# A decoder trunk of two layers: each reciprocal square root computed by one GpSimd instruction in place of eleven VectorE instructions

## The chip, the cores and the metric

The kernel runs on one core of one Trainium2 chip. The core has five engines that work side by side, each on its own queue of instructions and in the order of that queue: TensorE (PE; its weight loads stand apart as PEld), VectorE (DVE), ScalarE (ACT), GpSimd (POOL) and SyncE (SP), which here only issues transfers. They meet at semaphores. The metric is the device time of one execution in microseconds (us); lower is better.

## The reference, cut to what matters

A sequence of 256 tokens with 1024 features passes through two layers. Layer 0 mixes tokens by softmax attention heads (q and k normalised) and by Mamba-2 heads (a chunked scan, then a gated norm over groups of 512 features). Layer 1 mixes them by a gated delta rule (q and k normalised to length one, the output of each head normalised). After each mixer come a gated MLP with a short convolution, and an embedding that is gated by the sigmoid of a normalised residual. Each normalisation ends in one reciprocal square root:

```python
def rmsnorm(x, gain):
    xf = x.astype(jnp.float32)
    y = xf * lax.rsqrt(jnp.mean(xf * xf, axis=-1, keepdims=True) + EPS)
    return (y * gain.astype(jnp.float32)).astype(x.dtype)

def l2norm(x):
    return x * lax.rsqrt(jnp.sum(x * x, axis=-1, keepdims=True) + EPS)
```

The four other places (the group norm of the Mamba heads, the norm of a delta-rule head's output, and q and k in either layer) have the same form.

## The kernel before

All matrices stream once from memory, in blocks of up to 128 x 1024 numbers (`piece`, L133). ScalarE cuts each block to its high part (`whi`, L155), VectorE subtracts to get the low part (`wlo`, L156), and TensorE multiplies three times for each 128 x 128 tile and its 256 columns of activations (`mm3`, L174; L181 to L183). Four buffers each hold raw blocks, high parts and low parts. The residual `x` stays feature-major in eight tiles.

The norms are applied late. `norm_tile` splits `x` times the gain for the next product at once, while ScalarE squares the tiles and GpSimd adds the squares up (L241; in the very first norm VectorE does). `norm_end` (L244) sums over the partitions by four small matmuls into `nps`, VectorE scales (`st`, L251), `rsqrt` (L185) makes `rtok`, two numbers for each of 128 partitions, and two TensorE transposes (`rep`, L263) and a ScalarE copy spread it into `Rrep`, by which each product is multiplied when it leaves PSUM. So TensorE may go on with products before the norm is known, as far as its order of instructions lets it.

`rsqrt` takes the reciprocal square root of a small tile of 2, 4 or 32 columns: two integer instructions make a first guess (L189, L191), and three Newton steps of three instructions each follow (L197, L198, L199), all on VectorE and each needing the one before. It is called 25 times:

- six times in `norm_end`, with 2 columns: before layer 0, before and after each MLP, before layer 1;
- once in layer 0 for all q and k heads, with 32 columns (`_even`), and twice for the two groups of Mamba heads, with 2 columns;
- sixteen times in layer 1 (`_odd`), with 4 columns: eight times in `prep` for the lengths of k and q of a pair of heads (`rkq`), eight times in `core` for the output of the pair (`ro`).

In layer 1 `prep(kh)` projects and convolves q and k, transposes them (`pkq`), takes their squares, and builds from `rkq` the coefficients `cs`, the matrix `L` (VectorE L846, GpSimd L848, ScalarE L850) and its first inverse `T` (VectorE L854), which TensorE then transposes (`pS`, L858) and improves in six doublings and two Newton steps. `core(kh)` runs the two chunks, normalises the output (`so`, the rsqrt, `ro2`, `on`, `oT`), and `gate` multiplies it by the gate. Two pairs are prepared ahead of the one in `core`.

The order on each engine is not that of the code: the framework schedules all instructions by its own estimate of their durations and writes them into each engine's queue. The splits of weights stand ahead by a priority of 80 places. An engine then never passes over an instruction that waits. The six zero blocks `zb` for the doublings are filled on GpSimd early in layer 0 (L465).

Of the kernel before, what the change touches and what calls it, by code (L numbers as in the profile page):

```python
# [7 lines left out]
F32 = mybir.dt.float32  # L8
# [24 lines left out]
# Columns of the packed per-feature vectors (feature on the partition).  # L33
# [8 lines left out]
# Columns of the constants that depend on shapes alone.  # L42
# [8 lines left out]
class Trunk:  # L51
    def __init__(self, ctx, tc, stream, xT, pT, pv, tok, cst, out):
        self.tc, self.nc, self.ctx = tc, tc.nc, ctx
        self.stream, self.out = stream, out
        self.off = 0
        self.order = []
        self.n = 0
        self.pshare, self.share = 0.0, 0.0
        nc = self.nc
        ep = ctx.enter_context  # L60
        self.cpool = ep(tc.tile_pool(name="cpool", bufs=1))
        self.rawp = ep(tc.tile_pool(name="rawp", bufs=4))
        self.splp = ep(tc.tile_pool(name="splp", bufs=4))
        self.smallp = ep(tc.tile_pool(name="smallp", bufs=3))
        self.chain = ""
        self.nrm = ep(tc.tile_pool(name="nrm", bufs=1, space=PSUM))

        warm = self.cpool.tile([P, 1], F32, tag="warm", name="warm")
        nc.vector.memset(warm, 0.0)
        nc.scalar.activation(warm, warm, AF.Exp)  # L70
        # matmuls on zeros: TensorE's clock is up when the first operands arrive
        zt = self.cpool.tile([P, 256], F16, tag="zt", name="zt")
        nc.vector.memset(zt, 0.0)
        pz = self.nrm.tile([P, 512], F32, tag="nrm", name="pwarm")
        for _ in range(WARM):
            nc.tensor.matmul(pz[:, :T], zt[:, :P], zt, start=True, stop=True)
        self.pv = self.cpool.tile([P, NPV], F32, tag="pv", name="pv")
        nc.scalar.dma_start(self.pv, pv)
        xs = self.cpool.tile([P, KD, T], F32, tag="x", name="x")
        for m in range(0, KD, 2):  # L80
            nc.sync.dma_start(xs[:, m:m + 2], xT[:, m:m + 2])
        self.x = [xs[:, m] for m in range(KD)]
        self.tok = self.cpool.tile([P, 64], F32, tag="tok", name="tok")
        self.cst = self.cpool.tile([P, NCC], F32, tag="cst", name="cst")
        self.cst_src, self.tok_src = cst, tok
        self.pT = pT
        self.ones = self.cpool.tile([P, 1], F32, tag="ones", name="ones")
        nc.gpsimd.memset(self.ones, 1.0)
        self.ident = self.c("ident")
        self.id16 = self.cpool.tile([P, P], F16, tag="id16", name="id16")  # L90
        self.zb = [[self.cpool.tile([P, 4, P], F16, tag=f"zb{s}_{l}", name=f"zb{s}_{l}") for l in range(6)]
                   for s in range(1)]

# [13 lines left out]
    @contextmanager  # L107
    def psum(self, **banks):
        """The 8 PSUM banks of a phase, by the kind of work that rotates through them."""
        assert sum(banks.values()) <= 7  # L110
        with self.tc.tile_pool(name=self.uid("psum"), bufs=1, space=PSUM) as pool:
            self.psp, self.banks = pool, banks
            yield
# [12 lines left out]
    @contextmanager  # L126
    def on(self, chain):
        """Work of a chain of its own: its tiles don't wait for those of other chains."""
        was, self.chain = self.chain, chain
        yield  # L130
        self.chain = was

    def piece(self, blocks, lo=None):  # L133
        """Stream in weight blocks (array, layer, k0, nk, c0, nc), 1024 columns at a time, and split them."""
# [31 lines left out]
    def lo_engine(self, share):  # L166
        """GpSimd takes a share of the low halves, VectorE the rest."""
        self.pshare += self.share if share is None else share
        if self.pshare >= 1.0:
            self.pshare -= 1.0  # L170
            return self.nc.gpsimd
        return self.nc.vector

    def mm3(self, out, w, a, start=True, stop=True):  # L174
        """out += w.T @ a over k-tiles, w = (hi, lo) [128, nk, f], a = list of (hi, lo)."""
        nc = self.nc
        n = len(a)
        for k in range(n):
            wh, wl = w[0][:, k], w[1][:, k]
            ah, al = a[k]  # L180
            nc.tensor.matmul(out, wh, ah, start=start and k == 0, stop=False)  # L181
            nc.tensor.matmul(out, wh, al, start=False, stop=False)  # L182
            nc.tensor.matmul(out, wl, ah, start=False, stop=stop and k == n - 1)  # L183

    def rsqrt(self, src, n, dst=None):  # L185
        nc = self.nc
        s = self.small(n, "ri", I32)
# [15 lines left out]
    def split(self, src, hi, lo, scale=None):  # L203
        """hi + lo = src * scale, hi and lo of 12 significant bits."""
# [53 lines left out]
    def replicate(self, r, n, dst=None):  # L258
        """[128 tok, n] -> [128, n*128] with row values on every partition."""
# [92 lines left out]
    def conv4(self, pool, ps, w, b=None):  # L352
        """2 * silu(causal conv of R * ps), four taps, feature-major."""
# [20 lines left out]
    def softplus(self, x, n, dst):  # L374
        """max(x, 0) + log1p(exp(-|x|)) on a [128, n] tile; log1p by its atanh series."""
# [22 lines left out]
    def rowdram(self, col):  # L398
        """[128 tok, 32] -> [32, 128] in DRAM."""
# [15 lines left out]
    def _even(self, mp):  # L415
# [6 lines left out]
        # dt, decay sums  # L422
# [44 lines left out]
        # B, C, x  # L467
# [43 lines left out]
        def ssd(t):  # L511
            """heads 2t, 2t+1"""
# [28 lines left out]
        # q, k (feature-major), v (token-major)  # L541
# [69 lines left out]
        # attention  # L611
# [44 lines left out]
        # z gate, group norm  # L656
# [31 lines left out]
        # output projection  # L688
# [21 lines left out]
    def _odd(self, mp):  # L710
# [17 lines left out]
        # beta, decay sums  # L728
# [8 lines left out]
        # softplus(a + dt_bias) and softplus(-b) = -log(sigmoid(b))  # L737
# [47 lines left out]
        def prep(kh):  # L785
# [18 lines left out]
            # k stays as it is: 1 / |k| goes into the rows of the triangular system and its right sides,  # L804
            # and its solution times k needs none
# [10 lines left out]
            # Gram matrices  # L816
# [9 lines left out]
            # decays; index of a problem: chunk * 2 + head  # L826
# [25 lines left out]
            # inverse of the unit triangular L by doubling its blocks; T16 = inv(L), S16 = its transpose  # L852
# [36 lines left out]
            # two Newton steps in float32: S += S (I - L' S)  # L889
# [35 lines left out]
        def core(kh, st, bv):  # L925
            k2, qd, sq_, kt, Pm, S32, cs = st
            # chunk 0
# [10 lines left out]
            # chunk 1  # L938
# [11 lines left out]
            # outputs, token-major, index of a problem: chunk * 2 + head  # L950
# [7 lines left out]
            # normalisation over the value dim  # L958
# [198 lines left out]
```

## Time and profile before

| | us |
|---|---|
| median of 3 runs | 952.07 |
| the runs | 948.49, 952.07, 952.13 |
| span of the profiled execution, first to last instruction | 948.2 |
| TensorE busy | 903.1 (95%) |
| VectorE busy | 751.2 (79%) |
| ScalarE busy | 584.3 (62%) |
| GpSimd busy | 77.2 (8%) |

The profiled execution has a span and no device time of its own on record; its span is 0.3 under the fastest run and 3.9 under the median. The stages in the span: layer 0 mixer to about 205, MLP and embedding to 425, the delta rule to about 702, its output product, MLP and embedding to the end. A row of the timeline gives start, duration, engine, line, operation, result and operands, shape and number, and in brackets how long the engine had been idle and what it waited for. Rows of equal instructions that follow each other are merged ("x3").

### The profile page before, as it was taken

Reading aid. Unit: us, or ns where it says so; the run is one execution under the profiler, and the core shown is the slowest. Engines: PE = TensorE matmul, PEld = TensorE weight load, DVE = VectorE, ACT = ScalarE, POOL = GpSimd, SP = SyncE. Lnnn points to the kernel's source line nnn. Section 1 sums busy time; section 2 is a strip of 40 time slices with the busy share of each in tenths; the row PEclk is TensorE's granted clock in tenths of the full one; section 3 lists DMA queues with packets and bytes.
Section 4 is the critical chain, followed back from the end, with each engine's and each line's share of the span. In section 5 each row is a group of like instructions: output and inputs, shape, how many; then the busy total and the mean of one; then the engine's idle time right before and its main releaser. Section 6 shows DMA issues by size and latency. Waiting matters only on the chain.

```text
span 948.2 us, 19896 instructions
## 1 busy us (share of the span) xinstructions
PE 903.1 (95%) x7768; PEld 865.4 (91%) x7768; DVE 751.2 (79%) x1636; ACT 584.3 (62%) x1231; POOL 77.2 (8%) x83
## 2 busy tenths in 40 slices
PE   7979999999999999998989998999999999999998
PEld 5978778899999999987878898889899999999997
DVE  6767778888788766687889998999868888876665
ACT  5467656565655544664877777777745656654452
POOL 2000012110000001020111101111002000000100
PEclk9889999999999999999899999999999999999999
DMA  7544532456666555645333243322445555555562
GB/s 266 155 130 140 156 113 91 138 194 195 193 192 200 181 186 171 190 137 165 96 125 96 79 144 107 117 90 82 134 133 179 179 200 195 188 187 183 172 190 77
DMA packets 49822, 145.65 MB, mean 154 GB/s; under 512 B 9344, under 2 KB 15040, under 8 KB 49728
## 3 DMA queue, kind: packets, MB, share of 16 engines
q1 hardware_dynamic: 40608, 139.84, 46.7%
q10 hardware_dynamic: 9120, 4.53, 1.9%
q8 instruction: 61, 1.00, 0.4%
q14 instruction: 33, 0.27, 0.1%
HBM read 143.27 MB, written 1.08 MB: 152 GB/s over the span
## 4 chain that ended last, share of the span: by engine, by line
PE 75%; DVE 13%; DMA 4%; ACT 4%; issue 2%; POOL 1%; ACTq 0%; SPq 0%; POOLq 0%
PE pd L181 4%; PE pd L183 4%; PE pd L182 4%; PE pg L181 4%; PE pg L182 4%; PE pu L181 4%; PE pu L182 4%; PE pg L183 4%; PE pu L183 4%; DVE wlo L156 4%; DMA AC<-rowdr 2%; DMA GC<-rowdr 2%; PE pwo L182 2%; PE pgd L183 2%; PE pgd L181 2%
## 5 line engine op out<-in xcount | busy, mean ns | idle before, releaser
L156 DVE TENSOR_TENSOR wlo<-raw,whi 128x1024 fp32r<-128x1024 f32 (+2 forms) x266 | 323.5, 1217 | 89.1 <-ACT whi L155 85.6
L155 ACT ACTIVATE whi<-raw 128x1024 fp32r<-128x1024 f32 (+2 forms) x266 | 276.3, 1039 | 173.3 <-PE pd L182 46.3
L183 PE MATMUL pd<-yh,wlo 128*128 128x256 f32 x352 | 99.6, 283 | 0.0
L181 PE MATMUL pd<-yh,whi 128*128 128x256 f32 x352 | 99.6, 283 | 0.0
L182 PE MATMUL pd<-yl,whi 128*128 128x256 f32 x352 | 99.6, 283 | 0.0
L181 PE MATMUL pg<-xh,whi 128*128 128x256 f32 x352 | 97.3, 277 | 0.6 <-DVE x L1011 0.3
L181 PE MATMUL pu<-xh,whi 128*128 128x256 f32 x352 | 97.3, 277 | 0.0
L182 PE MATMUL pg<-xl,whi 128*128 128x256 f32 x352 | 97.3, 277 | 0.0
L183 PE MATMUL pg<-xh,wlo 128*128 128x256 f32 x352 | 97.2, 276 | 0.0
L182 PE MATMUL pu<-xl,whi 128*128 128x256 f32 x352 | 97.2, 276 | 0.0
L183 PE MATMUL pu<-xh,wlo 128*128 128x256 f32 x352 | 97.2, 276 | 0.0
L181 PE MATMUL pgd<-xh,whi 128*128 128x256 f32 x256 | 76.3, 298 | 0.3 <-DVE z L991 0.3
L182 PE MATMUL pgd<-xl,whi 128*128 128x256 f32 x256 | 74.9, 293 | 0.0
L183 PE MATMUL pgd<-xh,wlo 128*128 128x256 f32 x256 | 74.8, 292 | 0.0
L363 DVE SCALAR_TENSOR_TENSOR chh<-cg,pv,chh 128x255 f32<-128x255 f32 x132 | 66.7, 505 | 4.0 <-ACT chh L361 2.1
L183 PEld LDWEIGHTS pd<-yh,wlo 128*128 128x128 f32 x352 | 67.6, 192 | 0.0
L181 PEld LDWEIGHTS pd<-yh,whi 128*128 128x128 f32 x352 | 67.6, 192 | 0.0
L182 PEld LDWEIGHTS pd<-yl,whi 128*128 128x128 f32 x352 | 67.6, 192 | 0.0
L181 PEld LDWEIGHTS pg<-xh,whi 128*128 128x128 f32 x352 | 66.1, 188 | 0.8 <-issue 0.8
L182 PEld LDWEIGHTS pu<-xl,whi 128*128 128x128 f32 x352 | 66.1, 188 | 0.0
L183 PEld LDWEIGHTS pu<-xh,wlo 128*128 128x128 f32 x352 | 66.1, 188 | 0.0
L182 PEld LDWEIGHTS pg<-xl,whi 128*128 128x128 f32 x352 | 66.1, 188 | 0.0
(358 smaller groups left out, 2657.5 us busy)
## 6 DMA issues: line engine op xcount, KB each, us to landing
raw<-stream SPq DMA_DIRECT2D x232, 512.0 KB, 3.6
raw<-stream SPq DMA_DIRECT2D x32, 448.0 KB, 3.2
AC<-rowdr ACTq DMA_DIRECT2D x16, 128.0 KB, 4.0
GC<-rowdr ACTq DMA_DIRECT2D x16, 128.0 KB, 4.0
x<-xT SPq DMA_DIRECT2D x4, 256.0 KB, 5.0
out<-x SPq DMA_DIRECT2D x8, 128.0 KB, 1.8
cst<-cst SPq DMA_DIRECT2D x1, 645.0 KB, 6.4
raw<-pT SPq DMA_DIRECT2D x2, 256.0 KB, 2.5
```

The lines of the kernel that those rows point to most:

```text
L155: nc.scalar.activation(hi[:, :cols], raw[:, :cols], AF.Copy)
L156: self.lo_engine(lo).tensor_tensor(lo_[:, :cols], raw[:, :cols], hi[:, :cols].bitcast(F32), op=ALU.subtract)
L181: nc.tensor.matmul(out, wh, ah, start=start and k == 0, stop=False)
L182: nc.tensor.matmul(out, wh, al, start=False, stop=False)
L183: nc.tensor.matmul(out, wl, ah, start=False, stop=stop and k == n - 1)
L363: nc.vector.scalar_tensor_tensor(out=h[:, s:], in0=g[:, :T - s], scalar=w(3 - s), in1=h[:, s:], op0=ALU.mult, op1=ALU.add)
```

## The change

`rsqrt` issues one GpSimd `tensor_tensor` with the operation `pow` and returns; its second operand is a column of -0.5 that GpSimd writes once at the start. What stood in `rsqrt` before is no longer reached. The other differences are comments that were taken out; so line numbers rise by 2 after L88 and by 5 after `rsqrt`.

```diff
         self.ones = self.cpool.tile([P, 1], F32, tag="ones", name="ones")
         nc.gpsimd.memset(self.ones, 1.0)
+        self.mhalf = self.cpool.tile([P, 1], F32, tag="mhalf", name="mhalf")
+        nc.gpsimd.memset(self.mhalf, -0.5)
...
     def rsqrt(self, src, n, dst=None):
         nc = self.nc
+        o = dst if dst is not None else self.small(n, "ry")
+        nc.gpsimd.tensor_tensor(o, src, self.mhalf.to_broadcast([P, n]), op=ALU.pow)
+        return o
         s = self.small(n, "ri", I32)
         y = self.small(n, "ry")
```

The instructions of every engine are scheduled anew. Three places, each of before and then of after.

GpSimd, around the first norm (`rtok` is its result, `zb` the zero blocks, `xbc` a Mamba tile; the row `ISA` in the middle is a reload of GpSimd's instruction library, which the framework puts ahead of the first two-operand instruction):

```order
6 L88 MEMSET ones 128x1
7 L465 COPY zb_0_118<-id_117 128x512
8 L465 COPY zb_1_119<-id_117 128x512
9 L465 COPY zb_2_120<-id_117 128x512
10 L465 COPY zb_3_121<-id_117 128x512
11 L465 COPY zb_4_122<-id_117 128x512
12 L465 COPY zb_5_123<-id_117 128x512
13 L665 ISA
14 L665 TENSOR_TENSOR xbc_139_627<-xbc_139_627,z_451 128x256
```

```order
6 L88 MEMSET ones 128x1
7 L90 MEMSET mhalf 128x1
8 L470 COPY zb_0_120<-id_119 128x512
9 L470 COPY zb_1_121<-id_119 128x512
10 L470 COPY zb_2_122<-id_119 128x512
11 L190 ISA
12 L190 TENSOR_TENSOR rtok_259<-st_257,mhalf 128x2
13 L470 COPY zb_3_123<-id_119 128x512
14 L470 COPY zb_4_124<-id_119 128x512
15 L470 COPY zb_5_125<-id_119 128x512
```

The library load now stands directly ahead of the first `pow`, behind three of the six copies. On TensorE 22 more matmuls of the first z projection (`pz`) now stand ahead of the two `rep` transposes that wait for `rtok`; before, they stood behind them.

VectorE in the delta stage, around the norm of one pair's output (`st` are the small tiles ahead of the rsqrt and behind it, `cg` and `chh` steps of a convolution, `zb` a step of the doublings, `wlo` a low part):

```order
946 L970 TENSOR_SCALAR st_7689<-st_7687 128x4
947 L189 TENSOR_SCALAR ri_7691<-st_7689 128x4
948 L191 TENSOR_SCALAR ry_7692<-ri_7691 128x4
949 L197 SCALAR_TENSOR_TENSOR rt_7695<-ry_7692 128x4
950 L198 TENSOR_TENSOR rt_7696<-rt_7695,st_7689 128x4
951 L199 SCALAR_TENSOR_TENSOR ry_7697<-rt_7696,ry_7692 128x4
952 L197 SCALAR_TENSOR_TENSOR rt_7701<-ry_7697 128x4
953 L871 TENSOR_TENSOR zb_5_123<-pY_7433,cst 128x4x64
954 L198 TENSOR_TENSOR rt_7702<-rt_7701,st_7689 128x4
955 L363 SCALAR_TENSOR_TENSOR chh_7811<-cg_7809,pv,chh_7811 128x255
```

```order
747 L876 TENSOR_TENSOR zb_5_123<-pY_6657,cst 128x4x64
748 L972 SCALAR_TENSOR_TENSOR st_6911<-st_6904,st_6909 128x4
749 L975 TENSOR_SCALAR st_6913<-st_6911 128x4
750 L361 TENSOR_TENSOR cg_7266<-pgd_7241,Rrep_5420 128x256
751 L978 TENSOR_TENSOR st_6917<-ry_6915,sqs_6012 128x4
752 L376 SCALAR_TENSOR_TENSOR q_1409_6987<-cth_7020,chh_7015 128x256
753 L158 TENSOR_TENSOR wlo_7460<-raw_7457,whi_7459 128x1024
```

Before, the eleven steps are spread among the large instructions (the last of this rsqrt is row 962). After, the instruction that reads the result of `pow` (`st<-ry`) stands one instruction behind the one that makes its operand; over the sixteen calls of the stage there are none to three instructions between.

TensorE at the last norm (`nps` the sums over the partitions, `pgt` the gate product, `rep` the transposes that wait for `rtok`):

```order
7936 L248 MATMUL nps_13285<-ones,nss_13099 128x1
7937 L249 MATMUL nps_13285<-ones,nsq_13189 128x1
7938 L248 MATMUL nps_13285<-ones,nss_13099 128x1
7939 L249 MATMUL nps_13285<-ones,nsq_13189 128x1
7940 L181 MATMUL pgt_13331<-xh_12519,whi_13321 128x256
```

```order
7942 L254 MATMUL nps_12807<-ones,nsq_12711 128x1
7943 L183 MATMUL pgt_12833<-xh_12041,whi_12823 128x256
7944 L184 MATMUL pgt_12833<-xl_12042,whi_12823 128x256
7945 L185 MATMUL pgt_12833<-xh_12041,wlo_12824 128x256
7946 L183 MATMUL pgt_12833<-xh_12135,whi_12823 128x256
7947 L268 MATMUL rep_12817<-cst,rtok_12814 128x128 x2
```

Before, `rep` is row 7985: 45 matmuls stand between the sums and the transposes. After, there are four. The norm behind the first MLP and the one ahead of layer 1 have four as well (45 and 21 before), the two norms ahead of the MLPs nineteen, seven of them among the sums (33 before).

## Rows read from the trace of the kernel before

**Rows 1.** The page, busy time by engine: us (share of the span) xinstructions.

```profile
PE 903.1 (95%) x7768; PEld 865.4 (91%) x7768; DVE 751.2 (79%) x1636; ACT 584.3 (62%) x1231; POOL 77.2 (8%) x83
```

**Rows 2.** Windows: stretch, length, busy us of PE, PEld, DVE, ACT, POOL; clock, DMA.

```profile
205.00:385.00 180.00, 180.00 (x1559) 180.00 (x1559) 133.83 (x198) 99.94 (x149) 5.63 (x6) 1.00 0.59 186
...
425.00:702.00 277.00, 256.64 (x2480) 241.82 (x2480) 244.00 (x700) 200.91 (x562) 30.43 (x24) 0.98 0.37 111
```

**Rows 3.** Waits of PE, 425 to 702: waiter, awaited, us, times, longest.

```profile
PE pS L858 <- DVE T L854: 6.7, 7, 1.6
```

**Rows 4.** Timeline of VectorE, the first norm.

```profile
16.73 0.16 DVE L251 TENSOR_SCALAR st<-nps 128x2 f32<-128x2 f32 x1
...
21.80 0.16 DVE L199 SCALAR_TENSOR_TENSOR rtok<-rt,ry 128x2 f32<-128x2 f32 x1
...
28.62 0.42 DVE L486 TENSOR_TENSOR z<-pz,Rrep 128x256 f32<-128x256 f32 x1 [1.90 <-PE pz L183]
```

**Rows 5.** Timeline of GpSimd: three of six copies, and its first two-operand instruction.

```profile
15.55 3.75 POOL L465 COPY zb<-id 128x512 f16<-128x512 f16 x3 [14.72 <-ACT id L463]
...
64.06 0.99 POOL L665 TENSOR_TENSOR xbc<-xbc,z 128x256 f32<-128x256 f32 x1 [43.09 <-DVE xbc L538]
```

**Rows 6.** Timeline of PE, the first norm.

```profile
22.06 0.66 PE L263 MATMUL rep<-cst,rtok 128*128 128x128 f32 x2 [2.56 <-issue]
```

**Rows 7.** Windows behind the first norm, columns as in group 2.

```profile
22.00:26.00 4.00, 3.89 (x17) 3.59 (x18) 3.67 (x10) 2.05 (x4) 0.00 (x0) 0.50 0.41 141
```

**Rows 8.** The page, DMA issues: queue, count, KB each, median us to landing.

```profile
raw<-stream SPq DMA_DIRECT2D x1, 64.0 KB, 6.0
```

**Rows 9.** Timeline of ScalarE, its load of function tables.

```profile
1.17 1.28 ACT L70 ACT_TABLE_LOAD   x1 [1.17 <-PEq L1145]
```

**Rows 10.** Groups of GpSimd: form, count, busy us, mean ns, idle before.

```profile
L837 POOL TENSOR_TENSOR qd<-qd,q 128x256 f32<-128x256 f32 x8 | 6.2, 777 | 113.7 <-ACT qd L836 31.0 <-DVE q L371 25.9 <-DVE st L973 18.2
...
L88 POOL MEMSET ones<- 128x1 f32 x1 | 0.1, 98 | 0.3 <-POOLq L1145 0.3
```

**Rows 11.** Timeline of VectorE: steps of an rsqrt between large instructions, and in a chain.

```profile
497.30 0.16 DVE L198 TENSOR_TENSOR rt<-rt,st 128x4 f32<-128x4 f32 x1
497.37 0.16 DVE L191 TENSOR_SCALAR ry<-ri 128x4 int32<-128x4 int32 x1
...
551.25 0.17 DVE L189 TENSOR_SCALAR ri<-st 128x4 int32<-128x4 int32 x1
551.45 0.17 DVE L191 TENSOR_SCALAR ry<-ri 128x4 int32<-128x4 int32 x1
```

**Rows 12.** Timeline of GpSimd (first and third row) and of VectorE, delta stage.

```profile
474.70 1.28 POOL L848 TENSOR_TENSOR L<-L,cst 128x512 f32<-128x512 f32 x1 [15.05 <-DVE L L846]
...
474.88 2.18 DVE L156 TENSOR_TENSOR wlo<-raw,whi 128x1024 fp32r<-128x1024 f32 x1
...
570.78 2.53 POOL L848 TENSOR_TENSOR L<-L,cst 128x512 f32<-128x512 f32 x1 [14.04 <-DVE L L846]
```

**Rows 13.** Timeline of VectorE at the norm ahead of layer 1: first and last row.

```profile
421.60 0.16 DVE L251 TENSOR_SCALAR st<-nps 128x2 f32<-128x2 f32 x1 [1.18 <-PE nps L249]
...
424.03 0.16 DVE L199 SCALAR_TENSOR_TENSOR rtok<-rt,ry 128x2 f32<-128x2 f32 x1
```

**Rows 14.** Chain that ended last, 440 to 450: start, us, what.

```profile
442.47 6.90 DMA GC<-rowdr
```

**Rows 15.** Timeline of PE, then of VectorE, at the last norm.

```profile
919.68 0.36 PE L249 MATMUL nps<-ones,nsq 128*128 128x1 f32 x2
919.90 0.36 PE L181 MATMUL pgt<-xh,whi 128*128 128x256 f32 x1
...
920.08 0.16 DVE L251 TENSOR_SCALAR st<-nps 128x2 f32<-128x2 f32 x1 [1.42 <-PE nps L249]
```

**Rows 16.** Waits of the weight loads and of PE: waiter, awaited, us, times, longest.

```profile
PEld rep L263 <- issue: 5.2, 6, 2.7
...
PE pss L566 <- ACT sqk L563: 7.2, 3, 5.4
```

## The prediction

> **What bounds the kernel now.** I read the page first: TensorE is busy for 903.1 us of the span of 948.2, VectorE for 751.2, GpSimd for 77.2 [rows 1]. An average over stages says little, so the windows by stage come next. In the MLPs TensorE is busy for the whole stretch (180.00 of 180.00) and VectorE for three quarters of it; no reciprocal root stands there, and nothing can be won [rows 2]. In the delta stage, 425 to 702, TensorE is idle for 20.4 of 277 us and VectorE for 33.0: both are close to full, and sixteen of the 25 roots lie there [rows 2]. The waits of TensorE name what it is short of in that stage: 6.7 us, a third of its idle time, end on VectorE's `T`, which hangs on `rkq` [rows 3]. The other places are the six norms of the residual, where TensorE has to wait for `rep`. There it lost 5.2 us in all, 2.7 of them at the first norm [rows 16]. So TensorE sets the time, and a faster root is worth what it takes out of these waits: the waits for `T` and `rep`, and two long chains of small steps that start at a norm.
>
> **The part removed: eleven VectorE steps.** In a chain each starts 0.20 us behind the former; between large instructions a step pushes the next by 0.07 [rows 11]. There are 176 of them in the stage, and followed along the timeline they take 20.3 us of VectorE's queue, 0.115 each, so 1.27 for a root; the ends are 0.77 and 2.2.
>
> **The part added: one GpSimd `pow`.** The trace holds none. From below it costs a memset of one column, 0.10 us; from above the longest GpSimd row, 2.53 [rows 10, 12]. I take 0.78, the mean of the two-operand instruction of 256 columns, because the form is the same: far fewer columns speak for less, a power instead of a product for more [rows 10]. A handover costs 0.10: `rtok` ends at 21.96, `rep` starts at 22.06 [rows 4, 6]. To GpSimd and back a root takes 0.78 + 0.20 = 0.98 us.
>
> GpSimd also gets in VectorE's way. While it adds the identity to `L` (474.70, for 1.28), a subtraction `wlo` that started at 474.88 takes 2.18 us [rows 12]; it ends one ordinary subtraction after GpSimd does. I take it that a `pow` holds back in the same way what reads both operands from SBUF, as `wlo` does, and count only instructions that read PSUM as cover.
>
> At one place a rule of the Trainium skill speaks against the change: the page GPSIMD Engine Reference, section Engine selection, keeps two-operand elementwise work on VectorE, since GpSimd takes about twice as long. By that ratio on a step of 0.16 a `pow` would take an estimated 0.32, and the sum below would be some 5 us lower, not higher: the rule compares one instruction with one, and here one stands for eleven.
>
> **The delta stage.** VectorE's new order has none to three instructions between the operand and the reader of each root, 0.34 us on average over the sixteen, and I count half, 0.17, as cover. VectorE is thus held for 0.98 - 0.17 = 0.81 and freed of 1.27: 0.46 x 16 = 7.4 us of its queue. A third of TensorE's idle time ends on VectorE (6.7 of 20.4), so I pass on a third: -2.4. GpSimd's queue adds no wait that I can find: ahead of `rkq` stands `qd` of the same pair, which needs q, and so do the squares that `rkq` is made from. The chain from the squares to `T` gets shorter by about 6 us, but TensorE's order was written for that (some 60 matmuls between the last `pkq` and `pS` instead of some 100), so I count nothing for it.
>
> **The norm ahead of layer 1** starts the chain that ends in the landing of `GC` at 449.4, behind which TensorE is starved [rows 14]. From `st` to `rtok` it takes 421.76 to 424.19, 2.43 us [rows 13]; with `pow` 0.98. All of the 1.45 is on the path: -1.4.
>
> **The other norms.** Only four matmuls now stand between the sums and `rep` at three of them. At the last one the sums end at 920.04, `st` at 920.24, and the result would come at 921.22; four matmuls of 0.12 from 919.90 end by about 920.4 [rows 15]. TensorE idles 0.8 instead of the 0.5 of now ((5.2 - 2.7) / 5 [rows 16]): +0.9 for three. Two norms have twelve matmuls behind the sums, 1.4 us, which covers them: -1.0. Together -0.1. The roots of the attention and of the two groups lie beside other products; I count 0, with a us either way.
>
> **The first norm** is the place of the library load, which now stands right ahead of the first `pow`. Before, it had 43.09 us of idle time to hide in, so the trace bounds it by 0 and 43 [rows 5]. Two neighbours: a load of ScalarE's tables, 1.28 [rows 9], and a transfer of 64 KB from memory in these first microseconds, 6.0 [rows 8]. I take 6.0, since code for GpSimd has to come from memory. The copies end at 19.30 [rows 5], the load at 25.3, `rtok` at 26.1 instead of 21.96 [rows 4]. TensorE no longer loses the 2.56 at once, since 22 matmuls of `pz` stand ahead, but stops later all the same, and the granted clock of 0.50 (1.2 GHz) that followed the stop [rows 6, 7] comes again. Behind `rtok` hang the softplus, the decay sums and their trip through memory, at whose end TensorE waits 5.4 us [rows 16]. Part of the 4.1 us is made up, because VectorE had waited 1.90 for the second thing in that chain, the z product [rows 4], which is now partly done. Between 0 and +4.1 I take half: +2.0. With 1.28 instead of 6.0 `rtok` comes at 21.5, TensorE runs through at the higher clock (2.56, and some 26 matmuls at 0.12 instead of 0.21), and the term is -5.
>
> The Trainium skill has a price here: GPSIMD Engine Reference, section Instruction dispatch, puts the first call after such a load at about 6 us. By it the term stays at +2.0, and by the load of ScalarE's tables the whole sum would be 7 us lower. No row of this trace shows the load itself.
>
> **Sum:** -2.4 - 1.4 - 0.1 + 2.0 = -1.9 us, made against the span of 948.2. What lies around the span is not on record; the runs' median is 3.9 above it, and I carry the difference over to that: 952.1 - 1.9 = 950.2.
>
> **Rivals.**
> Slower: `pow` is long. Each further us costs 16 x 0.33 = 5.3 in the delta stage, 1 at layer 1, 3 to 5 at the other norms, about 0.5 at the first: some 11 us in all. From 0.78 + 0.6 = 1.4 us on the change is slower by more than 0.5%; at the 2.53 of the longest row it is +17, so 969. For it: a power is computed in many steps, and the scheduler left next to no cover. Against: GpSimd has only two to four columns to work on.
> Faster: the load is short, -5 for +2.0, so 943; or `pow` is close to the memset, -0.68 x 11 = -7.5, so 943 as well. For it: two columns are little work. Against: the transfers of that time are far from short.
> The roots were never what the delta stage waits for: its -2.4 falls away, 952.6. For it: the order on TensorE is fixed ahead, and one wait that ends sooner uncovers the next, ScalarE's at 73% of the stage [rows 2].
>
> **How the numbers follow.** A change of 0.5%, 4.8 us, is about what a measurement of this kernel can tell from none; the runs of before lie 3.6 apart. The forecast, with the third rival, which lies in the same band: 0.42. Slower: 0.28. Faster: 0.30. The likeliest time is 950.2, its own range 946 to 956. Cases of both signs hold more than half, so the range goes out to them: from 941 (the faster ones, less 2 for both together) to 967, which leaves out a `pow` of more than about 2.3 us, some 0.1, and 0.08 below.
>
> **What would show it.** The `pow` rows: 0.78 is the forecast, over 1.4 the slower rival. The first of them: its start at about 25.3, against 20.6 with a short load, and whether the clock of 22 to 30 us is still at 0.50. The idle time of TensorE ahead of `rep` at the last norm, 0.8. VectorE's busy share in 425 to 702 must fall, and its waits for GpSimd, which do not exist now, be about 0.8 for a root. The landing of `GC` must come 1.4 earlier relative to the norm. I am wrong in kind if TensorE's idle time in 425 to 702 falls by more than 8 us, or if GpSimd's queue holds a `pow` behind `qd` or `Ll`.

## The result and the profile after

The changed kernel takes 961.6 us (median of four runs, 958.2 to 964.4) beside 950.3 (946.4 to 952.1): a ratio of 1.0114, interval 1.0085 to 1.0143. It is slower by 1.1%, where 950.2 and no change were forecast. The profiled execution grew from 948.2 to 956.4 us.

What the edit says it does, it did. In the page's busy time, beside [rows 1], VectorE is freed and GpSimd loaded:

```profile
PE 901.4 (94%) x7768; PEld 862.9 (90%) x7768; DVE 722.3 (76%) x1361; ACT 584.9 (61%) x1231; POOL 114.0 (12%) x109
```

The `pow` rows, from the groups of GpSimd (form, count, busy us and mean ns, idle before it):

```profile
L190 POOL TENSOR_TENSOR rkq<-st,mhalf 128x4 f32<-128x4 f32 x8 | 8.9, 1110 | 37.8 <-DVE st L806 37.8
...
L190 POOL TENSOR_TENSOR ry<-st,mhalf 128x4 f32<-128x4 f32 x8 | 8.5, 1065 | 111.5 <-DVE st L975 111.5
...
L190 POOL TENSOR_TENSOR rtok<-st,mhalf 128x2 f32<-128x2 f32 x6 | 6.6, 1093 | 32.7 <-DVE st L256 32.7
...
L190 POOL TENSOR_TENSOR ry<-tss,mhalf 128x32 f32<-128x32 f32 x1 | 5.4, 5418 | 38.2 <-DVE tss L586 38.2
...
L190 POOL TENSOR_TENSOR ry<-st,mhalf 128x2 f32<-128x2 f32 x2 | 1.4, 706 | 0.9 <-DVE st L683 0.9
```

An undisturbed `pow` takes 0.70 us for two columns, 1.01 for four and 5.42 for 32, so some 0.15 for a column behind some 0.4 (an estimate from these three sizes). Who waited for these rows, from the view of line L190 (us, times):

```profile
  DVE st L978: 8.6, 8
  DVE cs L816: 6.3, 8
  PEld rep L268: 5.6, 4
  DVE rqk L588: 5.5, 1
```

The time did not go at one place. At GpSimd's first `xbc` product the changed kernel is 6.7 us ahead (64.1 to 57.4). At the first `nss` sum of the first MLP's norm it is 6.2 ahead (187.0 to 180.8), at the last `nss` ahead of layer 1 3.3 (418.2 to 414.9). At the first `nss` behind the delta stage it is 6.7 behind (713.1 to 719.8), at the end 8.2. So the start won some 6.5 us; the stretch with the first MLP and two norms gave back 2.9, the delta stage lost 10.0 and the last norm 1.5. In the MLP, 205 to 385, TensorE is busy throughout as before. The window of the delta stage, in the columns of [rows 2] (start and length first, clock third from the end), shows VectorE 19.8 us less busy, but TensorE less busy too: in the same 277 us fewer of its matmuls find room, 2401 instead of 2480.

```profile
425.00:702.00 277.00, 248.74 (x2401) 233.63 (x2400) 224.17 (x512) 197.31 (x557) 51.13 (x40) 0.98 0.36 108
```

To compare kernels I take the delta stage from the start of the last `nss` sum ahead of it to the start of the first behind it; every kernel has the same 2624 matmuls in it. Before, then after:

```profile
418.16:713.09 294.93, 274.01 (x2624) 258.62 (x2622) 257.19 (x733) 211.39 (x579) 31.16 (x26) 0.98 0.37 113
```

```profile
414.88:719.77 304.89, 275.68 (x2624) 259.79 (x2622) 241.93 (x546) 211.51 (x579) 52.74 (x42) 0.98 0.37 110
```

The waits of TensorE in that stage after the change (waiter, awaited, us, times, longest); the first answers to [rows 3], 6.7:

```profile
PE pS L863 <- DVE T L859: 13.3, 8, 2.7
PE pkq L800 <- DVE k L376: 4.7, 1, 4.7
PE oT L986 <- ACT on L982: 3.7, 5, 1.2
PE pvT L925 <- DVE v L376: 2.1, 3, 1.1
```

One pair of the stage shows how. Timeline of VectorE, GpSimd and TensorE, 524 to 533:

```profile
524.09 0.16 DVE L806 TENSOR_SCALAR st<-st 128x4 f32<-128x4 f32 x1
...
525.48 0.16 DVE L816 TENSOR_TENSOR cs<-hb,rkq 128x4 f32<-128x4 f32 x1 [0.90 <-POOL rkq L190]
...
530.99 1.37 DVE L859 TENSOR_TENSOR T<-L,sm 128x512 f16<-128x512 f16 x1
...
524.33 1.12 POOL L190 TENSOR_TENSOR rkq<-st,mhalf 128x4 f32<-128x4 f32 x1 [4.43 <-DVE st L806]
...
532.42 0.61 PE L863 MATMUL pS<-id,T 128*128 128x128 f16 x4 [2.69 <-DVE T L859]
```

The operand ends at 524.25, the root at 525.45, its reader starts at 525.48 after 0.90 us with nothing to do; `T` ends at 532.36 and TensorE has run out of other matmuls 2.69 us before it can start `pS`. For pairs two to eight `T` came 11 to 16 us behind `st` before the change; now it comes in 7.0 to 9.5. The chain is shorter, and TensorE meets it even sooner: in the order of the program 54 to 64 matmuls stand between the last `pkq` and the first `pS` of pairs three to eight, where 91 to 139 stood, and between `po` and `oT` 30 to 65 instead of 59 to 131.

### The profile page after: what moved, and what is told of

The parts are those of the page before. It is cut to its first block, busy times and chain, and to the rows that moved or that the text cites. A ratio compares the mean times of both kernels' runs of the same rounds, so it can differ in the third digit from the quotient of the medians.

```text
span 956.4 us, 19665 instructions
## 1 busy us (share of the span) xinstructions
PE 901.4 (94%) x7768; PEld 862.9 (90%) x7768; DVE 722.3 (76%) x1361; ACT 584.9 (61%) x1231; POOL 114.0 (12%) x109
## 4 chain that ended last, share of the span: by engine, by line
PE 61%; DVE 9%; ACT 4%; POOL 3%; issue 3%; DMA 1%; POOLq 0%; ACTq 0%
PE pg L183 4%; PE pd L183 4%; PE pd L184 4%; PE pd L185 4%; PE pg L184 4%; PE pg L185 4%; PE pu L185 4%; PE pu L183 4%; PE pu L184 4%; DVE wlo L158 2%; PE pgd L184 2%; PE pgd L183 2%; PE pgd L185 2%; PE pwo L184 1%; PE pwo L183 1%
## 5 line engine op out<-in xcount | busy, mean ns | idle before, releaser
L184 PE MATMUL pgd<-xl,whi 128*128 128x256 f32 x256 | 77.1, 301 | 0.0
L368 DVE SCALAR_TENSOR_TENSOR chh<-cg,pv,chh 128x255 f32<-128x255 f32 x132 | 70.6, 535 | 4.6 <-ACT chh L364 1.8
L185 PEld LDWEIGHTS pg<-xh,wlo 128*128 128x128 f32 x352 | 66.1, 188 | 0.0
```

The costliest lines, as they stand in the source:

```text
L368: nc.vector.scalar_tensor_tensor(out=h[:, s:], in0=g[:, :T - s], scalar=w(3 - s), in1=h[:, s:], op0=ALU.mult, op1=ALU.add)
```

## The experiments

Two theories and two rivals. **A**: the order was written for a root that costs next to nothing, so that a `pow` and its handover stand open in front of TensorE. **B**: the new order is worse whatever the root costs. **C**: the handover to GpSimd is what costs. **D**: GpSimd holds VectorE back, or its queue holds roots, in any order. To tell them apart, root and order are changed apart from each other. An order is held by edges between neighbours on the same engine, which set who is issued first and add no wait:

```diff
+    for a, b in zip(seq, seq[1:]):       # seq: the order of the other kernel, per engine
+        tc.add_manual_dep(ins[b], ins[a].name,
+                          mybir.DependencyInfo(mybir.DependencyClass.NoSync, ...), reason="order")
```

"Old order" is that of the kernel before, less the steps of its roots, "new order" that of the changed kernel, on TensorE, ScalarE and VectorE. Idle time is stage less busy time of TensorE. The ratio is against the kernel before, run beside it. Stage, busy and idle times come from the one profiled execution of each kernel, which took between 3.7 us less (e13) and 4.9 us more (e14) than that kernel's median; so stages that lie less than some 5 us apart are not told apart by them.

| kernel | root | order | stage | TensorE busy, idle | wait for T | median us, ratio (95%) |
|---|---|---|---|---|---|---|
| before | VectorE, 11 steps | old | 294.9 | 274.0, 20.9 | 6.7 | |
| after | pow | new | 304.9 | 275.7, 29.2 | 13.3 | 961.6, 1.0114 (1.0085 to 1.0143) |
| e1 | GpSimd product | new | 294.5 | 275.2, 19.4 | 11.6 | 945.2, 0.9966 (0.9939 to 0.9994) |
| e2 | pow | old | 291.5 | 273.3, 18.2 | 6.4 | 940.3, 0.9903 (0.9869 to 0.9938) |
| e5 | GpSimd product | old | 291.9 | 273.5, 18.3 | 6.7 | 938.3, 0.9865 (0.9827 to 0.9902) |
| e14 | one VectorE product | old | 297.2 | 276.0, 21.2 | 6.6 | 938.0, 0.9914 (0.9884 to 0.9943) |
| e8 | two pows | old | 297.5 | 276.1, 21.3 | 6.7 | 951.6, 0.9998 (0.9977 to 1.0019) |
| e7 | two pows | new | 328.7 | 284.7, 44.0 | 16.8 | 1005.5, 1.0576 (1.0526 to 1.0627) |
| e6 | VectorE, 11 steps | new | 332.1 | 287.4, 44.7 | 17.6 | 1008.5, 1.0613 (1.0563 to 1.0663) |

### The price of the root in the new order: e1

```diff
-        nc.gpsimd.memset(self.mhalf, -0.5)
+        nc.gpsimd.memset(self.mhalf, 0.01)
-        nc.gpsimd.tensor_tensor(o, src, self.mhalf.to_broadcast([P, n]), op=ALU.pow)
+        nc.gpsimd.tensor_tensor(o, src, self.mhalf.to_broadcast([P, n]), op=ALU.mult)
```

> The changed kernel with every pow replaced by a product of the same operands, tiles and form on GpSimd; the order on TensorE, VectorE, ScalarE and GpSimd is that of the changed kernel, instruction for instruction. The roots are left out of the result. Theory A (the order counts on a root that costs as little as a product; the pow, 1.0 to 1.1 us for four columns and 5.4 for 32, then stands open in front of TensorE): the product rows take 0.1 to 0.3 us, the delta stage gets the 10 us back that it lost, the attention 2 to 4, the last norm 1.5; 938 to 946 us. Theory B (the new order is worse in itself, whatever the root costs): at most the 4 to 5 us of attention and last norm come back, 951 to 957. Theory C (what costs is the handover to GpSimd and back, not the length of the pow): likewise 951 to 957, and the waits for GpSimd in the delta stage stay at more than half of the 14.9 us.

945.2 us, as A says; the attention's lead stays (its first `nss` is 9.3 ahead of before). The order did not even have to be held: built freely, the kernel with a product has the changed kernel's order row for row on every engine. What writes the order takes a `pow` for a product; on the chip the one takes 1.01 us and the other 0.20 for four columns, 5.42 and 0.24 for 32. The stage, and two of TensorE's waits in it:

```profile
411.18:705.69 294.51, 275.16 (x2624) 260.57 (x2622) 242.08 (x546) 211.05 (x579) 38.44 (x42) 0.98 0.37 114
```

```profile
PE pS L863 <- DVE T L859: 11.6, 8, 2.0
...
PE oT L986 <- ACT on L982: 0.7, 2, 0.4
```

From product to `pow`, all else equal, the stage grows by 10.4 us and the whole by 16.4. The wait for `T` is not where most of it lies: it is 11.6 us already with a product, by the order, and `pow` adds 1.7; of the 9.9 us of idle time that `pow` adds, 3.0 lie at `oT` and 1.8 at `pvT`. C falls: the handover is the same here, VectorE's waits for the output roots fall from 8.6 to 1.9 us, and those for `rkq` are not among the rows any more. B is not settled here; e5 shows its part.

### The old order with pow: e2

The changed kernel, held in the old order by the edges above; nothing else is edited.

> The changed kernel, pow for all 25 roots, but with every instruction of TensorE, ScalarE and VectorE held in the order of the kernel before (less the eleven steps of each root). Theory A: between the squares and pS stand some 100 matmuls again, which cover a pow of 1.1 us and its handover as they covered eleven steps of 1.3 to 2.2; the wait of TensorE for T is at or below the 6.7 us of before, the delta stage takes the 277 us of before or less, and with the start 6 us earlier the whole is 938 to 946 us. Theory B (order): the same, 938 to 946. Rival D (GpSimd's pow holds VectorE back, or its queue holds a root behind other work, in any order): the delta stage stays 5 us or more longer than before, 948 to 958.

940.3 us, faster than both kernels. Nobody waits for a `pow` in the delta stage now. The view of line L190 names, of those that waited, only readers of `rtok`, the root of a residual norm:

```profile
  DVE rr L581: 1.3, 1
  PEld rep L268: 0.7, 1
  DVE nr L745: 0.6, 1
  PE rep L268: 0.5, 1
```

The same pair as above (VectorE, GpSimd, TensorE):

```profile
515.94 0.16 DVE L806 TENSOR_SCALAR st<-st 128x4 f32<-128x4 f32 x1
...
520.63 0.15 DVE L816 TENSOR_TENSOR cs<-hb,rkq 128x4 f32<-128x4 f32 x1
...
516.18 1.22 POOL L190 TENSOR_TENSOR rkq<-st,mhalf 128x4 f32<-128x4 f32 x1 [2.43 <-DVE st L806]
...
527.21 0.40 PE L863 MATMUL pS<-id,T 128*128 128x128 f16 x4 [1.03 <-DVE T L859]
```

The root is ready at 517.40, its reader's turn comes at 520.63, 3.2 us later, and in the other seven pairs later still: the same instruction costs nothing. D falls with it.

### The other corners: e5 to e8

e5 is the edit of e1 held in the old order; e6 is the kernel before held in the new one. In e7 (new order) and e8 (old order) each root is done twice:

```diff
+        for _ in range(2):
             nc.gpsimd.tensor_tensor(o, src, self.mhalf.to_broadcast([P, n]), op=ALU.pow)
```

> The product instead of pow again (the roots are left out of the result), now in the order of the kernel before. In the new order the product ran the delta stage (last nss ahead of it to first nss behind it) in 294.5 us and pow in 304.9; in the old order pow took 291.5. Theory A (the old order covers a root of a microsecond): the cheaper root is worth next to nothing here, stage 290 to 292, whole 936 to 941. If the slope of the new order held here as well (10.4 us for the step from product to pow): stage 281, whole 928 to 931.

938.3 us, stage 291.9: in the old order the step from product to `pow` is worth nothing in the stage (291.9 and 291.5) and 2.0 us in the whole, where it is worth 10.4 and 16.4 in the new one. Beside e1, the same product in the new order, e5 is 6.9 us faster (5.9 in the profiled executions, 2.6 of them in the delta stage and 2.8 from the first `nss` of the first MLP's norm to the last ahead of layer 1). So B has a part too: of the 21.3 us between e2 and the changed kernel some 7 are the new order whatever the root costs, and some 14 the length of `pow` standing open in it.

> The kernel before, eleven VectorE steps for each root and nothing on GpSimd, with every instruction of TensorE and ScalarE, and VectorE's other instructions, held in the order of the changed kernel. Only the order is changed. Order as the cause: a root takes 2.2 us in a chain here, and the new order leaves it no cover, so the stage gets longer than the 304.9 of the changed kernel, 315 to 325 us, whole 965 to 985. If pow itself is the cause and the order is not: stage 292 to 297, whole 946 to 952.

The change of order alone, with the old roots: 1008.5 us, more than expected, 58 above the kernel before beside it. Its stage and the waits of TensorE in it:

```profile
429.11:761.22 332.11, 287.40 (x2624) 271.16 (x2622) 272.21 (x733) 212.18 (x579) 34.39 (x25) 0.94 0.33 100
```

```profile
PE pS L858 <- DVE T L854: 17.6, 8, 4.0
PE oT L981 <- ACT on L977: 9.2, 5, 2.3
PE pvT L920 <- DVE v L371: 5.3, 4, 2.3
```

TensorE idles 23.8 us longer than before, and its busy time for the same matmuls grows by 13.4, while the granted clock of the stretch goes from 0.98 to 0.94: more of the stretch ran at 1.2 instead of 2.4 GHz. Waits cost more than their own length here; in the changed kernel, with 8.3 us more of idle time, the clock stayed at 0.98. The expectation counted waits alone, and less the 13.4 the stage, 318.7, lies in its 315 to 325. Another 18.6 us were lost outside the stage (10.9 ahead of it, 7.7 behind it), which it did not count.

> The changed kernel in its own order, every pow done twice (same operands, same result), so that each root is about 1.05 us later for four columns, 5.4 later for 32. By the slope from product to pow in this order (10.4 us of stage for some 0.85 us of pow, 12 per us): stage 304.9 + 13 = 316 to 319, whole 970 to 980. If the pow's length is not what the new order waits for: within 3 us of 304.9, whole 956 to 966 (the 32 columns alone).

1005.5 us, stage 328.7: also more than expected: 9.05 us of it is TensorE's longer busy time (clock 0.95), and against the changed kernel another 17.1 us were lost ahead of the stage and 7.6 behind it. The slope grows with the length of the root: 10.4 us for the first 0.85, 23.8 for the next microsecond, the longer busy time included.

> Every pow twice in the old order. Two pows and two handovers take about 2.3 us, as eleven steps in a chain did (2.2). Theory A: the cover that stood behind eleven steps takes them, stage 292 to 296, whole 940 to 948. By the slope of the new order: stage 291.5 + 13 = 304, whole 953 to 957.

951.6 us. Between the two: the stage grew by 6.0 over e2, not by 23.8, and the wait for `T` hardly (6.4 to 6.7). The profiled execution grew from 937.1 to 952.0, and 8.8 us of that are there at the first `nss` of the first MLP's norm, behind the first norm and the 32 columns, which have no such cover.

### Where in the kernel: e3, e4, e11

```diff
-        nc.gpsimd.tensor_tensor(o, src, ..., op=ALU.pow); return o
+        if n != 4:          # e3: all but the delta stage; e4: n == 4, the delta stage alone
+            nc.gpsimd.tensor_tensor(o, src, ..., op=ALU.pow); return o
```

> pow for the nine roots outside the delta stage (six norms, attention, two groups), eleven VectorE steps for the sixteen in it. If the loss lies in the delta stage: the lead of 6 to 8 us of the first norm, less some 4 us in the attention, less 1 to 2 at the last norm, stays: 946 to 949 us. If the norms and the attention (1.8 us for a pow at two of the norms, 5.4 for 32 columns) carry it: 955 us or more.

949.1 us (0.9994, 0.9969 to 1.0019), at the edge of what was expected; the delta stage takes 291.9.

> pow for the sixteen roots of the delta stage alone. If the loss lies in the delta stage: 950 + 8 to 11 = 958 to 961 us, with TensorE waiting 12 to 15 us for T in that stage instead of 6.7. If it lies in the norms and the attention: 945 to 951.

964.4 us (1.0152, 1.0105 to 1.0198): the loss is in the delta stage and more than expected, 310.9 us with a wait for `T` of 10.8, less than the 12 to 15 expected. Both of these were ordered afresh, so they place the loss but don't size it.

```diff
+        if n == 4 and dst is None:      # ro: a product by one; new order held
+            nc.gpsimd.tensor_tensor(o, src, self.ones.to_broadcast([P, n]), op=ALU.mult)
```

> The changed kernel in its own order with pow everywhere but for the eight roots of the outputs (ro), which are products by one (left out of the result). Which of the two roots of a pair the new order waits for: if T alone (rkq), the stage stays within 2 us of 304.9, whole 958 to 962; if on and oT as well (3.7 us of waits, and the longer stay of what stands behind them), 298 to 302, whole 953 to 957.

958.8 us (1.0125, 1.0068 to 1.0181), stage 301.9. The time lies in the forecast for `T` alone, the stage in that for both. TensorE's idle time is 24.5 us, between the 29.2 with `pow` for both roots and the 19.4 with none, and the waits for `oT` fall from 3.7 to 0.7 while that for `T` stays at 13.4. So TensorE waits for both kinds of root; how the loss divides between them is not shown, since the profiled execution was 4.3 us longer than the median and the median is within the scatter of the changed kernel's.

### The start: e9, e10

In e9 the condition of e3's diff is that the root is the kernel's first.

> pow for the first norm alone, eleven VectorE steps for the other 24 roots. If the 6 to 7 us by which the first xbc product came earlier (64.1 to 57.4) are the first root's doing and stay to the end: 943 to 946 us. If later stages take them back, as they seemed to do for pow at all nine roots outside the delta stage (949): 948 to 951. If a first call of pow costs some us once, it is seen here alone: first xbc product at 60 or later.

942.7 us, 0.9971, but with an interval that reaches 1.0002; the trace, ordered afresh as well, keeps its lead from the first `nss` (7.1 us) to the end (8.4). The first `xbc` product comes at 59.97, at the mark that was set for a first call that costs; but the `pow` starts at 18.54, 0.06 behind the copies ahead of it, and takes the usual 0.70.

```diff
+    for i in zb:                         # e10: the kernel before, old order; six copies, behind xbc
+        tc.add_manual_dep(i, xbc[1].name, ..., reason="order")
```

> The kernel before, VectorE roots everywhere and its own order on TensorE, VectorE and ScalarE; only GpSimd's six copies of the identity (14.7 to 22.9 us, beside the first root) are put behind the second xbc product. If the first root was slow because GpSimd held VectorE's port (eleven steps in 5.0 us instead of 2.2): its steps take 0.16 to 0.2 each, rtok comes at 19.2 to 19.6 instead of 21.96, the half clock behind 22 us is gone, first xbc product at 57 to 60, whole 943 to 947. If the steps themselves are what is slow there: rtok within 0.5 of 21.96, first xbc at 63 to 65, whole 949 to 952.

944.4 us (0.9965, 0.9936 to 0.9993). Timeline of VectorE at the first norm, three of the root's steps:

```profile
18.37 0.16 DVE L191 TENSOR_SCALAR ry<-ri 128x2 int32<-128x2 int32 x1
18.57 0.16 DVE L197 SCALAR_TENSOR_TENSOR rt<-ry 128x2 f32<-128x2 f32 x1
...
20.13 0.16 DVE L199 SCALAR_TENSOR_TENSOR rtok<-rt,ry 128x2 f32<-128x2 f32 x1
```

In the kernel before, steps of this root took 0.51 to 0.57 us while the copies ran (18.20 to 20.98; the last copy ended at 20.97), and `rtok` ended at 21.96 [rows 4]; without them 0.16, and it ends at 20.29, somewhat later than I expected. The first `xbc` product comes at 58.7, and 5.6 us are still there at the last norm. The start's gain is thus no property of `pow`: small VectorE instructions beside GpSimd's copies were slow, and to move either away gives most of the same: at the first `nss` e10 is 5.2 us ahead, e9 7.1.

### Three more: e12, e13, e14

The order of e12 is that of a kernel whose root is six products of 256 columns in a chain and one of the root's own size; only the order is taken from it.

> pow for all roots, with TensorE, ScalarE and VectorE in an order that was written for a root of seven GpSimd products (six of 256 columns) instead of one: between the last pkq and pS stand 59 to 99 matmuls (in the changed kernel 54 to 64, in the kernel before 91 to 139), between po and oT 46 to 70 (30 to 44; 84 to 131). If the number of matmuls in between is what decides: stage 295 to 301, whole 944 to 953. If the old order is better for something else: 303 or more, whole 955 to 962.

949.5 us (1.0030, 0.9993 to 1.0067), stage 301.6. The wait for `T` falls to 7.6, and the idle time to 23.3, between new and old order as the number of matmuls is; but its busy time is 278.2 at a clock of 0.97, and other waits came up. The time is inside one forecast, the stage just outside it: the number of matmuls explains `T`, not the whole stage.

```diff
-        nc.gpsimd.tensor_tensor(o, src, ..., op=ALU.pow); return o
+        if n != 32:                      # e13, in the old order, the copies issued late as in e10
+            nc.gpsimd.tensor_tensor(o, src, ..., op=ALU.pow); return o
```

> The order of the kernel before, pow for 24 roots, VectorE's eleven steps for the one of 32 columns, and GpSimd's copies of the identity behind the second xbc product. Nothing stands ahead of the first pow, so a load of its code, if it takes time, is seen here: first pow at 17.0 if it is free, at 18.3 or later otherwise. If the gains add (5 us at the start from the copies, 3 us in the delta stage from the order with pow, up to 2 in the attention from the 32 columns): 936 to 940 us. If the start's gain and the attention's don't add: 940 to 943.

940.8 us (0.9928, 0.9904 to 0.9953): the gains of the start and of the order don't add beyond e2. It also shows a first `pow` with nothing ahead of it on GpSimd, 0.15 us behind its operand (16.46), and `MODIFY_POOL_CONFIG`, the row of the library load, at 0.8 us. This `pow` takes 1.56 instead of 0.70, beside a `wlo` that had started at 16.39:

```profile
16.61 1.56 POOL L191 TENSOR_TENSOR rtok<-st,mhalf 128x2 f32<-128x2 f32 x1 [15.75 <-DVE st L257]
```

```diff
-        nc.gpsimd.tensor_tensor(o, src, self.mhalf.to_broadcast([P, n]), op=ALU.pow)
+        nc.vector.tensor_scalar(out=o, in0=src, scalar1=0.01, scalar2=None, op0=ALU.mult)
```

> One VectorE product in the place of each root (the roots are left out of the result), in the order of the kernel before, nothing added on GpSimd: what VectorE's freed queue alone is worth. If the 3.4 us that pow won in the delta stage in the old order (294.9 to 291.5) came from VectorE's queue: stage 291 to 293. If GpSimd's taking part had a hand in it (port, handover): below 290 here. The wait for T stays at 6.4 to 6.9 us in either case if no root lies in it. Whole 937 to 945.

938.0 us, inside the forecast, but the stage, 297.2, is outside both. So the stage's 3.4 us from 294.9 to 291.5 are no proof of what VectorE's freed queue is worth: in the old order the stage takes 291.3 to 297.5 us for five kinds of root, in no order of their cost, and it is long where TensorE's wait for the first `k` is long (5.8, 6.0 and 5.6 us at 294.9, 297.2 and 297.5; 3.8, 4.2 and 2.9 at 291.5, 291.9 and 291.3). But e10, at 294.5 with a wait of 4.3, does not fit. More likely the stage varies from one execution to the next: the profiled execution of e14 took 942.9 us, 4.9 above its median, and is level with e5's up to the last `nss` ahead of the stage (409.1 in both). What can be told apart is the whole: with the root's eleven steps and the start mended 944.4 (e10), with `pow` 940.3, with one instruction 938.0.

## Why the prediction was wrong, point by point

**What bounds the kernel.** TensorE does. But the sentence that a third of its idle time ends on `T`, "which hangs on `rkq`", was the first error. In the old order that wait is 6.7, 6.4, 6.7, 6.6 and 6.7 us for eleven steps, `pow`, product, one step and two `pow`s. No root lies in it. A row of waits names who came last, and whether a shorter root would have moved it could be seen only behind `rkq`: its reader in e2 has its turn 3.2 us or more after the root is done. The third rival said as much.

**The steps removed.** VectorE's busy time in 425 to 702 falls from 244.0 to 224.2 us, but that window no longer holds the same work. Over the whole stage it falls by 15.3 (257.2 to 241.9), in e2 by 16.8; 20.3 had been counted, gaps in the chains included. Nearly right.

**The price of `pow`**, 0.78: 0.70 for two columns, but 1.01 for four, 30% more, and of sixteen roots none has two. The row of 256 columns was no measure, since a `pow` goes by its columns, at some 0.15 each. For the 32 columns the price was outside my bounds (5.42 above 2.53) and had been counted 0, "with a us either way"; VectorE waits 5.5 us for it, and the first `nss` behind it is 6.2 us ahead of the kernel before, against 9.3 with a product. The handover of 0.10 was right (0.08 and 0.03 in the pair above), and VectorE's waits, 6.3 and 8.6 us for eight roots each, are near the 0.8 for a root that was named as a sign.

**GpSimd in VectorE's way.** The other way round. No VectorE instruction beside a `pow` was lengthened, but a `pow` was where a `wlo` starts at the same time. Timeline of GpSimd, then of VectorE, at the last norm:

```profile
927.05 1.78 POOL L190 TENSOR_TENSOR rtok<-st,mhalf 128x2 f32<-128x2 f32 x1 [12.09 <-DVE st L256]
...
927.04 2.36 DVE L158 TENSOR_TENSOR wlo<-raw,whi 128x1024 fp32r<-128x1024 f32 x2
```

1.78 instead of 0.70, as at 387.69. The Trainium skill (SBUF — State Buffer, section Who interferes with whom) says that a VectorE instruction with two SBUF inputs contends with a GpSimd instruction that reads SBUF, and that the order of issue decides which of the two is held up. The trace agrees in these two places, where `wlo` starts 0.01 us earlier or in the same hundredth, and in e13, where it starts 0.22 earlier. Where the `pow` is first the runs do not bear it out: the `wlo` at 19.77, inside the `pow` from 19.54, takes its usual 1.22, and in e2 two that start inside the `pow` of 32 columns (109.64, for 5.66), at 110.06 and 113.81, take 1.23 and 1.22. Why is not shown. The `wlo` in the changed kernel:

```profile
19.77 1.22 DVE L158 TENSOR_TENSOR wlo<-raw,whi 128x1024 fp32r<-128x1024 f32 x1 [0.77 <-ACT whi L157]
```

**The delta stage**, -2.4: it became +10.0, and this is the step that failed and decided the outcome: the shorter cover on TensorE was put at nothing. The prediction saw that the order on TensorE had changed ("some 60 matmuls between the last `pkq` and `pS` instead of some 100") and that the chain was shorter by 6 us, and counted nothing for the two together, as if they cancelled. In this stage they do for a root that costs what the order assumes, as in e1: 294.5. The root's time beyond that finds little cover, and each pair's chain shows it: from product to `pow`, `st` to the end of `T` grows by 0.31 to 0.82 us for pairs two to eight. To pass on a third had no ground in the old order, which passes on nothing (291.5 and 291.9); in the new one some three quarters are passed on, 10.4 us of stage for 16 roots that are each some 0.85 longer (13.6), and from both kinds of root, as the waits for `T`, `oT` and `pvT` show.

**The norm ahead of layer 1**, -1.4. From the last `nss` to the first `qd` it is 1.7 us shorter after; but in e10, with VectorE's steps, 1.3. Open.

**The other norms**, -0.1. At the last norm TensorE waits 1.54 for `rep`, against 0.8 forecast, by the `wlo` above; the end is another 1.5 us late. In e1 the product there took 1.27 beside the same `wlo`, and TensorE waited 1.0. The mechanism was right, the price was not. The stretch with the first MLP and two norms gave back 2.9 us, where a gain of 0.1 had been expected from these norms and the last together; a product in the new order gives back 2.4 there, so most of it is the order and not `pow`.

**The first norm**, +2.0: it became -6.7. No time for a load of code was seen: in the changed kernel the first `pow` starts at 19.54, right behind three of the copies, instead of at 25.3, and the clock in 22 to 30 us stays up, where it had been 0.50 from 22 to 26 [rows 7]. The `pow`, and the window:

```profile
19.54 0.70 POOL L190 TENSOR_TENSOR rtok<-st,mhalf 128x2 f32<-128x2 f32 x1
```

```profile
22.00:30.00 8.00, 7.60 (x66) 7.42 (x66) 7.52 (x25) 4.84 (x8) 0.58 (x2) 1.00 0.60 211
```

The prediction cited the Trainium skill for about 6 us (GPSIMD Engine Reference, section Instruction dispatch); the changed kernel does not show them, and in e13, where 15.75 us of idle time lie ahead of the first `pow`, a load would not be seen unless it were longer. I had bounded the load by neighbours that were loads of another kind [rows 8, 9], and did not see in [rows 4] that the steps were slow because of the copies in [rows 5].

**The rivals.** The slower one came true in sign, but before its point: `pow` did not have to pass 1.4 us. Its slope of 11 us per us of `pow` was for the old order's way of passing on; measured in the new order, product to `pow` costs 16.4 us for 0.85 at four columns, 0.5 at two and 5.2 at the one root of 32. The range, wide enough for both signs, held the time; the sign and the account behind it did not. Of the 3.9 us carried over from the span to the median 1.8 are what lies around the span, in the later runs as well, and the rest is scatter between executions; that moved the number by 2 us, not the sign.

## What to carry to other kernels

When an edit changes an instruction's engine or count, the scheduler rewrites the order for the price it believes, and a price that is too low takes the cover away: the edit and the new order are two changes, to be measured apart. Count the work that stands between a producer and its reader on the bounding engine before and after, and set it against the whole chain at measured prices; where the cover shrinks with the chain, most of what the price was wrong by is paid in time (here some three quarters). The new order cost some 7 us here even for a root as cheap as assumed (e1 beside e5). Holding the old order kept the good of this edit: `pow` at 0.9903 instead of 1.0114.

## What was not expected of the hardware

A `pow` on GpSimd costs 0.70, 1.01 and 5.42 us for 2, 4 and 32 columns, against 0.19, 0.20 and 0.24 for a product of the same form. The first `pow` of the changed kernel starts 0.06 us behind the copies ahead of it and takes the usual 0.70, so nothing is visible of a price for its code. A two-column `pow` that starts with a `wlo` takes 1.78, but a `wlo` that starts inside a `pow` takes its usual 1.22. And more waits can come with a lower clock: in the stage of e6 23.8 us more of idle time came with 0.94 instead of 0.98 of the clock and 13.4 us more of busy time for the same matmuls.
